# Eight-core decoder trunk: the second token pair's input in eight parts during the first down projection, its norm in the second gate/up, modulation rows paused there, the start modelled with 295 GB/s

## The chip, the cores and the metric

The kernel runs on all 8 cores of one Trainium2 chip, one program for all, each core with one sequence of the batch. The metric is the device time of the slowest core in microseconds (us), over several executions. Cores 0 to 3 are one die, cores 4 to 7 the other. For every execution the span of each core and its mean granted TensorE clock are known (1.0 is full speed); a profile exists for one execution of each kernel.

Executions differ. In most, all cores are within some 10 us of one another. In others some cores run at a lower granted clock and take longer (in the first profile here 1960.5 to 1963.5 us at a mean clock of 0.968 to 0.970, beside 1931.2 to 1935.7 us at 0.985 to 0.990); such cores always came in pairs here, (0,1), (2,3), (4,5) or (6,7), one pair or two. I call an execution **undisturbed** when it is below 1950 us, **short episode** when its slowest core is between 1950 and 2010 us, and **long episode** above 2040 us; nothing lies between 2010 and 2040. Long episodes come with the kernel before and with most of the others here, and no time difference is explained with them. Many short episodes count as "fast" in the ratios (they are within 1.5% of the fastest run), others as slow; I therefore list executions singly where it matters.

## The reference

Two layers, each of three sub-layers (SwiGLU, token mixer, SwiGLU), every one behind an RMSNorm with a shift, scale and gate from a conditioning vector. Only the first SwiGLU matters here (shortened):

```python
D_MODEL = 1024; BATCH = 8; SEQ = 2048; DEPTH = 2; D_FF = 2816
def modulate(x, g, mod):
    shift, scale, gate = jnp.split(mod, 3, axis=-1)
    return rmsnorm(x, g) * (1.0 + scale[:, None, :]) + shift[:, None, :], gate[:, None, :]
def swiglu(h, w_in, w_out):
    g, u = jnp.split(h @ w_in, 2, axis=-1)
    return (jax.nn.silu(g) * u) @ w_out
def reference(...):
    c_act = jax.nn.silu(c)
    for l in range(DEPTH):
        mod = c_act @ w_mod[l] + b_mod[l]               # the "modulation rows"
        h, gate = modulate(x, norm_g[l, 0], mod_f1)
        x = x + 0.5 * gate * swiglu(h, w_ffn_in[l, 0], w_ffn_out[l, 0])
        ...                                             # mixer, second SwiGLU
    return rmsnorm(x, final_g)
```

## The kernel before

The kernel is generated: a scheduler in Python simulates five engines and one shared DMA wire, gives every operation a modelled start, and each engine's program is its operations in the order of these starts. (`L465` in the views is the line of the helper that records every operation, so go by the names of the tiles.) At the end, VectorE, ScalarE and TensorE are ordered once more by `relist`, a list schedule by due time.

The sequence of 2048 tokens is four tiles of 512 (`X[:, t]`), worked on in two pairs. A phase is one sub-layer for one pair; the SwiGLU's 22 blocks of 128 hidden channels go in two groups (12 and 10): gate/up, down, gate/up, down. Weights stream through six slots (`SLOTS`) in pieces of 512 KB. The matrices are multiplied by a scheme with 7 instead of 8 products, which needs sums of weight blocks: VectorE makes them when a piece has landed.

```python
    def piece_sums(pc):                      # VectorE: four sums per weight piece
        ...
        tt_(v(4), v(3), v(2), ALU.add, [k(2), k(3)], [k(4)], half=True)
        tt_(v(3), v(0), v(3), ALU.subtract, [k(0), k(3)], [k(3)], half=True)
        ...
    def rows_pump():                         # one modulation row per 8 ticks, if VectorE has slack
        row_tick[0] += 1
        if row_tick[0] >= ROW_EVERY and slack():
            ...
    Sd.BW = 320e3                            # modelled bandwidth of the start, bytes/us
    ...                                      # start: CT, SM, CB, 12+4 rows, X of the first pair, norm
    for n in range(WARM):                    # WARM = 36: matmuls on idle TensorE at the start
        op = mm(PS[5][:], ONES[:], SQ[:, n % NSQ, :], True, True, ...)
        op.after = 28.0 + n * 0.6
    ...
    Sd.BW = Sched.BW                         # the rest is modelled with another figure
    ...
    def late_x():                            # X of the second pair: two loads of 2 MB
        for t in range(2, 4):
            add("sp", I("dma_start", out=X[:, t, :, :], in_=xT[t]...), reads=[("A", ablk(6, 0))], ..., dma=("X", t))
    ...
                if k == 0 and g == 0:        # first gate/up of the first phase
                    run_segs(segs[:X_AT])    # X_AT = 55
                    late_x()
                    bg_add(stats_gen([2, 3]))    # squares and their sums over channels, for the norm
                    run_segs(segs[X_AT:-3])
                ...
                if g == 0:                   # at the start of the down projection
                    late_norm = pm is not None
                    rstd(other, after=Sd.tl["pe"].tail())   # the norm's roots
                ...
                if not last:
                    run_down(dn, rest)
```

## Time and profile before

| kernel before, first chip | us |
|---|---|
| time, median of 3 executions | 1965.8 (1965.01 to 1966.27) |
| profiled execution: cores 2 to 5 | 1931.2 to 1935.7 |
| profiled execution: cores 0, 1, 6, 7 | 1960.5 to 1963.5 |

The prediction below shows the spans, the slices and the chain. Two more views of core 7 belong to it. TensorE's waits over the whole run (what it waited for; us in total, times, longest):

```profile
PE ps L465 <- ACT SQ L465: 24.9, 2, 19.6
PE ps L465 <- DMA ACTB<-wmod: 4.3, 1, 4.3
PE ps L465 <- DVE TP L465: 3.7, 1, 3.7
```

The first two belong to the start, before there is anything to multiply. The third, one wait of 3.7 us at 123.5 us, is the only large one in the remaining 1900 us. The DMA transfers issued from 105 to 140 us (count, size of one, median us from issue to landing):

```profile
X<-xT SPq DMA_DIRECT2D x2, 2048.0 KB, 19.4
SLOTS<-wout POOLq DMA_DIRECT2D x4, 512.0 KB, 16.1
```

Pieces of down weights (`wout`) that land in 5.3 us in the median of the whole run take 16.1 us beside the two loads of X.

### The profile page before, as it was taken

The page shows a single profiled execution, that of the slowest core. Times are in us where ns is not written, and L with a number is a line of the kernel's source. Part 1 is how long each engine was busy: PE and PEld are TensorE (multiplying, and loading weights), DVE is VectorE, ACT ScalarE, POOL GpSimd, SP SyncE. Part 2 cuts the span into 40 slices and gives each one's busy share as a digit, 9 for nine tenths or more (in the row PEclk, how much of TensorE's full clock was granted, in tenths as well). Part 3 has the DMA queues.
Part 4 walks back from the last instruction along what each step waited for, and adds up shares of the span by engine and source line. Part 5 has one row for each costly group of instructions (what it writes and reads, how often), then busy time and mean ns, then how long its engine had stood idle before and what let it go on. Part 6 is the DMA issues. An engine that isn't in the chain of part 4 may idle for free.

```text
span 1963.5 us, 25398 instructions; the slowest of 8 cores (1931.2 to 1963.5 us)
## 1 busy us (share of the span) xinstructions
PE 1909.8 (97%) x8706; PEld 861.4 (44%) x8706; DVE 1697.0 (86%) x3256; ACT 1031.9 (53%) x1738; POOL 172.4 (9%) x330
## 2 busy tenths in 40 slices
PE   3999999999999999999999999999999999999997
PEld 1534444444444444444444444444444444444443
DVE  4778889999798999999988888898998889988865
ACT  4454455456564555565455544564466555574343
POOL 0000000000202000000000000000000000000000
PEclk6898889999999999999999999999999999999999
DMA  9795748787777768686855454555454444445752
GB/s 271 148 222 121 151 87 182 145 178 155 155 167 175 160 150 183 144 171 122 182 100 89 82 90 77 96 96 87 75 90 67 85 85 86 76 76 86 174 87 94
DMA packets 66653, 248.72 MB, mean 127 GB/s; under 512 B 7520, under 2 KB 7648, under 8 KB 66016
## 3 DMA queue, kind: packets, MB, share of 16 engines
q0 software_dynamic: 42192, 153.64, 46.9%
q1 hardware_dynamic: 24336, 93.45, 14.7%
q8 instruction: 74, 1.21, 0.2%
q14 instruction: 51, 0.42, 0.1%
HBM read 392.29 MB, written 8.39 MB: 204 GB/s over the span
## 4 chain that ended last, share of the span: by engine, by line
PE 91%; DMA 4%; DVE 3%; ACT 1%; SPq 1%; issue 0%; DVEq 0%; POOLq 0%
PE ps L465 91%; DMA ACTB<-wmod 2%; DMA SLOTS<-wout 1%; DVE X L465 1%; SPq L465 1%; DMA SLOTS<-win 1%; DVE WMOD L465 0%; DVE ACTB L465 0%; DVE TP L465 0%; DVE SLOTS L465 0%; ACT PMH L465 0%; ACT ps L465 0%; DVE ps L465 0%; ACT L465 0%; ACT TP L465 0%
## 5 line engine op out<-in xcount | busy, mean ns | idle before, releaser
L465 PE MATMUL ps<-H,SLOTS 128*128 128x512 f16 x5440 | 1214.9, 383 | 9.0 <-DVE TP L465 3.7
L465 PEld LDWEIGHTS ps<-H,SLOTS 128*128 128x128 f16 x5440 | 534.5, 99 | 667.5 <-issue 71.6
L465 ACT ACTIVATE ps<-ps 128x512 f32<-128x512 f32 x684 | 397.8, 582 | 595.0 <-PE ps L465 558.4
L465 PE MATMUL ps<-ACTB,SLOTS 128*128 128x512 f16 x2780 | 628.5, 385 | 0.3
L465 PEld LDWEIGHTS ps<-ACTB,SLOTS 128*128 128x128 f16 x2780 | 274.9, 99 | 339.4 <-issue 46.6
L465 DVE TENSOR_TENSOR SLOTS<-SLOTS 128x512 f16<-128x512 f16 x996 | 393.4, 417 | 17.5 <-DMA SLOTS<-wout 7.7
L465 DVE SCALAR_TENSOR_TENSOR X<-ps,GH,X 128x512 f32<-128x512 f32 x424 | 308.3, 744 | 49.5 <-PE ps L465 45.5
L465 ACT ACTIVATE TP<-ps 128x512 f32<-128x512 f32 x400 | 238.2, 596 | 131.9 <-PE ps L465 130.1
L465 DVE TENSOR_TENSOR ACTB<-TP,ps 128x512 f16<-128x512 f32 x368 | 248.1, 683 | 43.1 <-PE ps L465 28.5
L465 ACT ACTIVATE SQ<-X 128x512 bf16<-128x512 f32 x224 | 131.2, 623 | 103.6 <-DVE X L465 55.3
L465 POOL DMA_DIRECT2D SLOTS<-win x176 | 93.1, 530 | 1047.1 <-PE ps L465 971.5
L465 DVE TENSOR_TENSOR TP<-ps,TP 128x512 f32<-128x512 f32 x176 | 120.9, 687 | 55.0 <-ACT ps L465 54.0
L465 DVE SCALAR_TENSOR_TENSOR WMOD<-WMOD,CB 128x1024 f32<-128x1024 f32 x130 | 157.6, 1216 | 1.9 <-DMA WMOD<-wmod 1.8
L465 DVE TENSOR_TENSOR TP<-X,RS 128x512 f32<-128x512 f32 x192 | 128.5, 683 | 11.4 <-ACT ACTB L465 8.3
L465 DVE TENSOR_TENSOR ps<-ps,TP 128x512 f32<-128x512 f32 x176 | 122.2, 694 | 16.0 <-PE ps L465 15.2
L465 DVE TENSOR_TENSOR ACTB<-ACTB 128x1024 f16<-128x1024 f16 (+1 forms) x188 | 104.2, 564 | 1.4
L465 POOL DMA_DIRECT2D SLOTS<-wout x88 | 46.5, 528 | 516.9 <-PE ps L465 516.9
L465 PE MATMUL ps<-SQ,ONES 128*128 128x512 bf16 x166 | 58.9, 438 | 28.9 <-ACT SQ L465 24.9
L465 ACT ACTIVATE H<-TP,MODT,AS 128x512 f16<-128x512 f32 x81 | 62.9, 807 | 20.7 <-DVE TP L465 13.8
L465 ACT ACTIVATE PMH<-TP,MODT,AS 128x512 f16<-128x512 f32 x60 | 47.7, 807 | 19.1 <-DVE TP L465 19.0
L465 ACT ACTIVATE ACTB<-TP,MODT,AS 128x512 f16<-128x512 f32 x51 | 40.9, 809 | 14.9 <-PE ps L465 12.0
L465 DVE TENSOR_TENSOR SQ<-SQ 128x1024 bf16<-128x1024 bf16 (+1 forms) x56 | 36.3, 647 | 11.9 <-ACT SQ L465 11.5
(74 smaller groups left out, 538.7 us busy)
## 6 DMA issues: line engine op xcount, KB each, us to landing
SLOTS<-win POOLq DMA_DIRECT2D x176, 512.0 KB, 6.2
WMOD<-wmod SPq DMA_DIRECT2D x131, 512.0 KB, 5.5
SLOTS<-wout POOLq DMA_DIRECT2D x88, 512.0 KB, 5.3
SLOTS<-wab POOLq DMA_DIRECT2D x28, 512.0 KB, 8.9
X<-xT SPq DMA_DIRECT2D x4, 2048.0 KB, 21.0
outT<-X SPq DMA_DIRECT2D x16, 512.0 KB, 3.7
ACTB<-wmod SPq DMA_DIRECT2D x13, 512.0 KB, 28.2
CB<-cb SPq DMA_DIRECT2D x1, 512.0 KB, 6.1
```

Of the source, the lines that this page charges most:

```text
L465: return lambda E: getattr(E, name)(*a, **k)
```

## The change

The intent, read from the diff: load X of the second pair where there is more room, in parts that follow TensorE's progress; make its norm where it does not stand in the way; keep VectorE and DMA free of modulation rows in the meantime; and model the start with 295 instead of 320 GB/s. The whole diff:

```diff
--- before.py
+++ after.py
@@ -21,7 +21,7 @@
 EPS = 1e-6
 NSLOT = 6
 STAGE = True
-X_AT = 55
+R_AT = 21
 WARM = 36
 SLG = (2, 3, 4, 6, 7, 7)
 
@@ -843,12 +843,13 @@
 
     row_queue = []
     row_tick = [0]
+    rows_on = [True]
     ROW_EVERY = 8
     SLACK = 3
 
     def rows_pump():
         row_tick[0] += 1
-        if row_tick[0] >= ROW_EVERY and slack():
+        if row_tick[0] >= ROW_EVERY and rows_on[0] and slack():
             row_tick[0] -= ROW_EVERY
             while row_queue and row_queue[0] in done_rows:
                 row_queue.pop(0)
@@ -1489,7 +1490,7 @@
 
 
 
-    Sd.BW = 320e3
+    Sd.BW = 295e3
     add("sp", I("dma_start", out=CT[:], in_=ct_d), writes=["CT"], cost=0.06, dma="CT", nbytes=128 * 32)
     add("sp", I("dma_start", out=SM[:], in_=small_d), writes=["SM"], cost=0.06, dma="SM", nbytes=128 * SM_N * 4)
     add("sp", I("dma_start", out=CB[:], in_=cb_d), writes=["CB"], cost=0.06, dma="CB", nbytes=128 * 4096)
@@ -1614,9 +1615,15 @@
     carry = []
 
     def late_x():
+
         for t in range(2, 4):
-            add("sp", I("dma_start", out=X[:, t, :, :], in_=xT[t].rearrange("p (c k) -> p c k", k=TT)), reads=[("A", ablk(6, 0))],
-                writes=[Xk(c, t) for c in range(NC)], cost=0.06, dma=("X", t), nbytes=128 * 16384)
+            for c in range(0, NC, 2):
+                last = max(o.idx for o in Sd.ops[-60:] if o.eng == "pe")
+                op = add("sp", I("dma_start", out=X[:, t, c:c + 2, :], in_=xT[t][:, c * TT:(c + 2) * TT].rearrange("p (c k) -> p c k", k=TT)),
+                         writes=[Xk(c, t), Xk(c + 1, t)], cost=0.06, dma=("X", t, c), nbytes=128 * 4096, after=Sd.tl["pe"].tail())
+                op.deps.add(last)
+                yield
+                yield
 
     def run_segs(segs, side=iter(())):
 
@@ -1644,6 +1651,7 @@
         nxt = PHASES[k + 1] if k + 1 < len(PHASES) else None
         other = [2, 3] if p == 0 else [0, 1]
         t_begin = Sd.tl["pe"].tail()
+        rows_on[0] = True
         if sub[0] == "F":
             l, i = sub[1], sub[2]
             s = 2 * i
@@ -1663,11 +1671,12 @@
                 segs = [f for _, f in gu_segments(units)]
                 first, rest = dn.segments(segs[-3:])
                 late = last and late_norm
-                if k == 0 and g == 0:
-                    run_segs(segs[:X_AT])
-                    late_x()
-                    bg_add(stats_gen([2, 3]))
-                    run_segs(segs[X_AT:-3])
+                if k == 0 and g == 1:
+                    run_segs(segs[:R_AT])
+                    bg_drain()
+                    rstd(other, after=Sd.tl["pe"].tail())
+                    bg_add(early_h(sub, nxt))
+                    run_segs(segs[R_AT:-3])
                 else:
                     run_segs(segs[:-3])
                 if not late:
@@ -1680,7 +1689,10 @@
                     bg_drain()
                     rstd(other, after=Sd.tl["act"].tail())
                 pm = {("F", 1, 0, 1): 0, ("F", 1, 1, 0): 1}.get(sub + (p,)) if g == 0 else None
-                if g == 0:
+                if g == 0 and k == 0:
+                    late_norm = False
+                    rows_on[0] = False
+                elif g == 0:
                     late_norm = pm is not None
                     rstd(other, after=Sd.tl["pe"].tail())
                 if pm is not None:
@@ -1694,8 +1706,10 @@
                 if g == 0 and nxt is None:
                     bg_add(final_gen(0))
                 if not last:
-                    run_down(dn, rest)
-                    if not late_norm and nxt is not None and STAGE:
+                    run_down(dn, rest, late_x() if k == 0 else iter(()))
+                    if k == 0:
+                        bg_add(stats_gen([2, 3]))
+                    elif not late_norm and nxt is not None and STAGE:
                         carry.append(lambda sub=sub, nxt=nxt: bg_add(early_h(sub, nxt)))
                 elif nxt is not None:
                     run_down(dn, rest, side)
```

## The prediction

> **What bounds the kernel now.** I read the spans of the cores first, because the time is that of the slowest core; then the page's forty slices; then TensorE's waits; then a timeline and stretches of 2 us around the one place that stood out. The cores:
>
> ```profile
> core 4: 1935.7 us, clock 0.990
> core 5: 1933.5 us, clock 0.985
> core 6: 1961.4 us, clock 0.968
> core 7: 1963.5 us, clock 0.970
> ```
>
> Cores 0, 1, 6 and 7 take 1960.5 to 1963.5 us, cores 2 to 5 take 1931.2 to 1935.7 us, with the same program. The page (core 7) says what the work is:
>
> ```profile
> PE   3999999999999999999999999999999999999997
> PEclk6898889999999999999999999999999999999999
> PE 91%; DMA 4%; DVE 3%; ACT 1%; SPq 1%; issue 0%; DVEq 0%; POOLq 0%
> ```
>
> TensorE is full from the second slice to the last but one, and is 91% of the chain. So only three things can shorten the run: less idle time of TensorE, a higher clock, or an earlier start. The clock is below full at the start and in slices 3 to 6 (98 to 295 us). Core 7 there, in stretches (columns: TensorE busy, weight loads, VectorE, ScalarE, GpSimd, granted clock, DMA share, GB/s):
>
> ```profile
> 100.00:120.00 20.00, 20.00 (x95) 9.09 (x93) 19.08 (x41) 9.63 (x17) 1.58 (x3) 1.00 0.97 209
> 120.00:140.00 20.00, 16.28 (x67) 6.66 (x66) 11.54 (x25) 10.65 (x21) 1.06 (x2) 0.89 1.00 262
> 140.00:160.00 20.00, 19.78 (x76) 7.87 (x75) 16.70 (x34) 13.37 (x24) 1.05 (x2) 0.81 0.61 139
> 280.00:300.00 20.00, 20.00 (x81) 8.43 (x80) 16.73 (x32) 5.47 (x10) 1.05 (x2) 0.85 0.49 105
> ```
>
> Between 120 and 140 us TensorE loses 3.7 us, DMA is at 1.00, and from about 137.7 us the clock is 0.81 until about 296.3 us; then it is 1.00 to the end. Core 5 shows 1.00 in all four of these stretches. [...] What happened at 120 to 128 us, in the timeline of core 7:
>
> ```profile
> 111.14 0.53 POOL L465 DMA_DIRECT2D SLOTS<-wout  x1 [5.52 <-PE ps L465]
> 111.39 0.81 SPq L465 DMA_DIRECT2D X<-xT  x2
> ...
> 126.09 0.42 DVE L465 TENSOR_TENSOR SLOTS<-SLOTS 128x512 f16<-128x512 f16 x1 [5.13 <-DMA SLOTS<-wout]
> 126.44 0.68 DVE L465 TENSOR_TENSOR TP<-ps,TP 128x512 f32<-128x512 f32 x1
> ...
> 127.26 9.83 PE L465 MATMUL ps<-H,SLOTS 128*128 128x512 f16 x37 [3.72 <-DVE TP L465]
> ```
>
> The two 2 MB tiles of the second pair are issued at 111.39 us. The piece of down weights issued 0.25 us before takes 14.9 us to land (the page's median is 5.3). VectorE, in order, sits 5.13 us before the first weight sum of that piece; the addition behind it is what TensorE waits for. So the load starves the weights, VectorE passes the wait on, and TensorE stops. On cores 0, 1, 2, 6 and 7 the clock then falls to 0.50 for some 5 us; on core 7 it is back at 1.00 by 132 us, and 0.81 follows some 6 us later.
>
> [...] the eight cores ran dense at 1.00 from 68 to 122 us and again from 296 us to the end, and only one episode of 159 us came, on the cores 0, 1, 6, 7. It looks like an answer to the restart, not to the load. [...]
>
> **The change, part by part.**
>
> *Load of X.* The two 2 MB transfers at 111 us go; eight of 512 KB come during the first down projection, one for two products, issued as TensorE advances. A product is 6 matmuls of 0.213 us (94 in 20 us at full clock), 1.28 us, so a part comes each 2.6 us. At 324 GB/s (93.45 MB of that queue in 14.7% of the span) a part takes 1.6 us of all DMA engines: a share of 0.6 for 20 us. The rows that are paused there took 512 KB in some 7 us, a share of 0.23. The unthrottled core 5 has a mean DMA share of 0.73 from 150 to 200 us, so the sum is about 1.1 for 20 us in the first two thirds of the down, where few weight pieces are released, then less. Landing times will rise to perhaps 10 us; weights loaded there are for the gate/up after it, over 20 us away. I expect no stall of TensorE.
>
> What is saved: the sum of (length minus busy time x clock) in stretches of 2 us from 118 to 148 us is 5.5 us on core 2, 3.1 on core 3, 3.7 on core 4, 3.4 on core 5; on core 7 it is 6.2 up to 132 us. If the stall goes, so does the restart, and I expect the 29.7 us on the four cores to go with it.
>
> *Norm.* The 16 squares (0.62 us) now fall in the down, where ScalarE has only some ten copies of 0.58 us to make. Their order on ScalarE leaves each part about 9 us from its issue to the copy behind it, so a landing up to 9 us holds up nothing. The roots (two of 0.72, two of 0.6 us, two table loads of 1.28) move from the start of the down, where no SiLU is wanted, into the second gate/up. Together about 5.2 us in which no SiLU can run, with TensorE's banks held meanwhile: my estimate is 0 to 2 us of TensorE wait.
>
> *Rows.* None are made from the first down to the end of the first phase; they are made up in the next phase, where VectorE has little room (busy 48.7 of 50 us from 300 to 350 us on core 5, though overlapping records overstate that). The instruction order shows the same 50 rows loaded before the mixer starts. The scheduler puts them behind what TensorE waits for: 0 to 1 us.
>
> *Start.* The modelled bandwidth of the start is 295 instead of 320 GB/s. No transfer changes, but orders do. Of the 36 warming matmuls, 14 stood behind the late row (TensorE waits 4.3 us for it, then runs at clock 0.50 without a gap up to the first real matmul at 63.8 us); now 10 do. Each costs 0.38 us there: 4 x 0.38 = 1.5 us earlier on every core.
>
> *Sum.* Cores 2 to 5: 1935.6 - 5.5, 1931.2 - 3.1, 1935.7 - 3.7, 1933.5 - 3.4 give 1930.1, 1928.1, 1932.0, 1930.1. Core 7: 1963.5 - 29.7 - 6.2 = 1927.6. The slowest less the start's 1.5 us: 1930.5; plus about 1 us for the norm and the rows: 1931.5. The timed figure was 1.5 us above the span in the profiled execution (1965.01 and 1963.5): 1933.
>
> **Rivals.** (a) The limit is tripped anyway, by the hot start or by the denser DMA in the down: for it speaks that no one knows what trips it; against it, that the start at 66 us ramped all cores up with no such answer. Then about 29 us stay on some cores: 1933 + 29 = 1962 at most, some 1957 where the stall's own cost falls away. I give this 0.22. (b) The root block in the gate/up stops TensorE for over 3 us, with a cold clock after it: 3 to 6 us, or a new trip. For it: six banks and a SiLU in each unit; against: copies run in between and the scheduler counted the block. (c) The eight parts delay a weight piece as before, now at the turn to the second gate/up: 2 to 4 us. Against: issue is spread by TensorE's progress. (d) The start gains more than I count: if TensorE stayed warm through the late row, the chain behind it (14.3 us at half clock) would shrink by up to some 5 us, and the time would be 1927. Against: core 6 waited only 2.6 us for that row and still ran at 0.50.
>
> **Range and chances.** No trip and 1925 to 1940: about 0.75. Trip, 1952 to 1963: 0.22. For 8 in 10 the range has to reach into the second: 1924 to 1959. Faster by over 2% means below 1926.5, which takes 6.5 us more than I can find: 0.14. Slower by over 2%: 0.01.
>
> **What would show it.** In the new profile: no wait of TensorE over 1 us after the start; weight landings of at most some 10 us; clock 1.00 on all cores from about 67 us on, and cores within 5 us of one another. The first real matmul near 62.3 us on core 7. I am wrong if 0.81 appears with no stall before it (then the load, not the restart, trips the limit), if the clock falls after the root block near 210 us, or if the cores start much earlier.

"The limit", there and below, is only a name for the granted clock of 0.81; what imposes it was not shown. The working of the 29.7 us used the clock to more digits than the traces give; from the traces it is an estimate of 158.6 us (137.7 to 296.3) x 0.19 = 30.1 us, or 29.3 to 30.9 for a clock of 0.805 to 0.815, and core 7's sum becomes 1927.2 instead of 1927.6. The forecast itself comes from core 4, 1935.7 - 3.7 = 1932.0, less 1.5, plus 1, is 1931.5, and 1933 as timed. Two readings are put right here: on cores 0, 1, 2, 6 and 7 the clock of 0.50 lasted 3.3 to 3.4 us (stretches of 0.5 us), not some 5; and of the eight cores at 1.00 from 68 to 122 us core 4 had 0.99, with TensorE busy for 53.3 of the 54 us.

## The result and the profile after

| | before | after |
|---|---|---|
| time, median of 4 executions each | 1966.03 us | 1937.55 us (1935.16 to 1940.84) |
| ratio after/before, 95% interval | | 0.9857 (0.984 to 0.9874) |
| profiled execution, slowest core | 1963.5 us | 1933.5 us |

The result is correct against the reference. All ratios are the mean time of one kernel's fast runs over that of the other's fast runs of the same rounds, so not quite the ratio of the medians quoted. This is 1.4% faster. The time is 4.6 us above the prediction (1933), inside its range; the profiled execution is the fastest of the four (1935.16).

The spans after (profiled execution):

```profile
core 3: 1933.5 us, clock 0.993
...
core 6: 1932.5 us, clock 0.986
core 7: 1927.7 us, clock 0.993
```

The two groups of cores are gone. Core 7 is 35.8 us shorter than before, core 3 is 2.3 us longer. From the page of core 3, the slices of the granted clock and the chain that ended last:

```profile
PEclk9899999999999999999999999999999999999999
...
PE 88%; DMA 4%; DVE 3%; ACT 2%; SPq 1%; issue 1%; POOL 0%; DVEq 0%
```

After the start the clock is at full: from 68 us to 1900 us every core has a mean of 1.00 in stretches of 56 us and more, and no core has a stretch at 0.81. Two of the stretches of core 7 that the prediction shows (the same columns), now:

```profile
120.00:140.00 20.00, 20.00 (x94) 9.08 (x93) 19.11 (x43) 9.30 (x16) 1.59 (x3) 1.00 0.80 189
140.00:160.00 20.00, 20.00 (x94) 9.11 (x93) 17.56 (x34) 5.60 (x10) 1.05 (x2) 1.00 0.88 199
```

94 matmuls in 20 us at clock 1.00, against 67 and 76 before. And the timeline of core 7 there, where the kernel before had 5.13 us of waiting on VectorE and 3.72 us on TensorE:

```profile
120.78 0.69 DVE L465 TENSOR_TENSOR TP<-ps,TP 128x512 f32<-128x512 f32 x1
...
124.39 0.75 DVE L465 TENSOR_TENSOR SLOTS<-SLOTS 128x512 f16<-128x512 f16 x2
```

No wait stands behind either line. But a second thing differs, and the prediction had not looked for it: the addition (`TP<-ps,TP`, which frees a bank for TensorE) now stands *before* the weight sums (`SLOTS<-SLOTS`). In the kernel before it stood behind one, at 126.44. What did it: the missing load, or the order?

The new places. The parts of X lie in the first down projection; transfers of core 3 issued from 145 to 190 us:

```profile
X<-xT SPq DMA_DIRECT2D x7, 512.0 KB, 10.4
SLOTS<-win POOLq DMA_DIRECT2D x7, 512.0 KB, 10.6
WMOD<-wmod SPq DMA_DIRECT2D x5, 512.0 KB, 12.1
```

The load is thinner but the weights and rows beside it are late (`win` lands in 5.7 us and `wmod` in 5.9 us in the median of the whole run), and on some cores this reaches TensorE. Core 5, timeline (the bracket is the engine's idle time before the line, and what ended it):

```profile
163.87 0.42 DVE L465 TENSOR_TENSOR SLOTS<-SLOTS 128x512 f16<-128x512 f16 x1 [5.26 <-DMA SLOTS<-win]
...
165.10 10.52 PE L465 MATMUL ps<-ACTB,SLOTS 128*128 128x512 f16 x48 [2.10 <-DVE X L465]
...
208.90 3.40 PE L465 MATMUL ps<-H,SLOTS 128*128 128x512 f16 x15 [0.59 <-DVE ps L465]
```

VectorE sits 5.26 us before a weight sum whose piece is late, and the update of X behind it holds up TensorE for 2.10 us: the old mechanism on a smaller scale, at another place. The last line is all that the norm's roots cost in the second gate/up. On core 3, a modulation row does the same:

```profile
186.37 1.22 DVE L465 SCALAR_TENSOR_TENSOR WMOD<-WMOD,CB 128x1024 f32<-128x1024 f32 x1 [3.13 <-DMA WMOD<-wmod]
...
188.35 1.02 PE L465 MATMUL ps<-H,SLOTS 128*128 128x512 f16 x4 [1.98 <-DVE TP L465]
```

The pause is not complete: from 145 to 290 us core 3 still makes 9 rows, against 19 in the kernel before and 16 without the pause (experiment 3); 5 of the 9 lie before 190 us.

### The profile page after: what moved, and what is told of

It reads as the page before. It is cut to its first block, busy times and chain, and to the rows that moved or that the text cites. A ratio compares the mean times of both kernels' runs of the same rounds, so it can differ in the third digit from the quotient of the medians.

```text
span 1933.5 us, 25425 instructions; the slowest of 8 cores (1927.7 to 1933.5 us)
## 1 busy us (share of the span) xinstructions
PE 1880.4 (97%) x8706; PEld 853.4 (44%) x8706; DVE 1694.7 (88%) x3256; ACT 1030.3 (53%) x1738; POOL 174.6 (9%) x330
## 4 chain that ended last, share of the span: by engine, by line
PE 88%; DMA 4%; DVE 3%; ACT 2%; SPq 1%; issue 1%; POOL 0%; DVEq 0%
PE ps L465 88%; DMA WMOD<-wmod 3%; DMA SLOTS<-win 1%; SPq L465 1%; DVE WMOD L465 1%; DVE SLOTS L465 1%; DVE ACTB L465 1%; DVE TP L465 1%; DVE X L465 0%; ACT ps L465 0%; ACT PMH L465 0%; DVE ps L465 0%; ACT ACTB L465 0%; ACT TP L465 0%; ACT L465 0%
## 5 line engine op out<-in xcount | busy, mean ns | idle before, releaser
L465 PE MATMUL ps<-H,SLOTS 128*128 128x512 f16 x5440 | 1199.7, 379 | 9.3 <-ACT ps L465 3.3
L465 PE MATMUL ps<-ACTB,SLOTS 128*128 128x512 f16 x2780 | 613.8, 379 | 0.1
```

The lines of the kernel that those rows point to most:

```text
L465: return lambda E: getattr(E, name)(*a, **k)
```

## The experiments

My theory after the result was that of the prediction: the 4 MB load makes the stop, the stop makes the restart, and the restart trips the 0.81 limit. Rivals: the limit is tripped by something else (the load itself, or chance), and another part of the change removed the stop. Twelve runs of ten kernels were made, on four further chips, called B, C, D and E here; all gave correct results. Each kernel was timed against the kernel before on its chip, except `stall8` (one look).

### 1. Only the start's modelled bandwidth (chip B)

```diff
 # kernel before
-    Sd.BW = 320e3
+    Sd.BW = 295e3
```

> The kernel before with only the start's modelled bandwidth changed (295 instead of 320 GB/s). My theory (the start gains 1.5 us, the rest comes from the stall at 122 to 127 us and the limit that follows it): first real matmul on core 7 near 62.1 us instead of 63.8, the stall and the 0.81 episode of some 159 us remain, 1964 us. Rival (the start is what matters): no episode, about 1938 us.

Measured: 1935.85 us median of 5 executions; four at 1934.9 to 1935.9, one at 1963.31 with cores 6 and 7 long. Ratio 0.9911 (0.9819 to 1.0003; the interval is wide because executions of before with short episodes count as fast). The expectation fell. X is still two loads of 2 MB at 110.84 us, and `wout` pieces still land late, in 15.3 us in the median; yet core 7 has no stop of TensorE (the longest wait there on any core is 0.90 us):

```profile
120.68 0.69 DVE L465 TENSOR_TENSOR TP<-ps,TP 128x512 f32<-128x512 f32 x1
...
124.53 0.76 DVE L465 TENSOR_TENSOR SLOTS<-SLOTS 128x512 f16<-128x512 f16 x2 [0.16 <-DMA SLOTS<-wout]
```

The addition stands before the weight sums, as in the changed kernel. The order of the program was changed by nothing but a modelled time of the start. So the start's "no transfer changes, but orders do" had a consequence 60 us later that the prediction had not looked at.

### 2. All of the change but the start's bandwidth (chip B)

```diff
 # changed kernel
-    Sd.BW = 295e3
+    Sd.BW = 320e3
```

> The changed kernel with the start's modelled bandwidth as before (320 GB/s). My theory: no stall over 2.5 us at 120 to 200 us, clock 1.00 after 68 us on all cores, only the start comes 1.7 us later: 1939 us. Rival (the start is what matters): the episode is back, about 1965 us.

Measured: 1939.2 us median of 4 (1936.12, 1938.13, 1940.27, and one long episode, 2188.37). Ratio 0.992 (0.9763 to 1.0076), by itself unclear. As expected: no stop at 124 us and no short episode. The order is still the old one, the sum ahead of the addition, but with no load of X beside it the piece is there in time (`wout` lands in 7.4 us in the median from 105 to 140 us); core 7:

```profile
121.27 0.41 DVE L465 TENSOR_TENSOR SLOTS<-SLOTS 128x512 f16<-128x512 f16 x1
121.60 0.68 DVE L465 TENSOR_TENSOR TP<-ps,TP 128x512 f32<-128x512 f32 x1
```

TensorE waits at most 0.74 us there on any core (core 1). So the two halves of the change each remove the stop, one by moving the load, the other by accident of order. The expected limit of 2.5 us for stalls up to 200 us did not hold, nor the clock of 1.00: the waits in the down are larger here, and core 3 shows 0.71 from 190 to 194 us (4 matmuls take 1.02 us at 190.46 us and 1.86 us at 191.66 us):

```profile
188.48 1.23 DVE L465 SCALAR_TENSOR_TENSOR WMOD<-WMOD,CB 128x1024 f32<-128x1024 f32 x1 [3.93 <-DMA WMOD<-wmod]
...
190.46 1.02 PE L465 MATMUL ps<-H,SLOTS 128*128 128x512 f16 x4 [3.86 <-DVE TP L465]
```

### 3. The change without the pause of the rows (chip B)

```diff
 # changed kernel
-                    rows_on[0] = False
```

> The changed kernel with the modulation rows not paused. My theory: some 20 rows more before 300 us, DMA in the first down at 1.00 for longer, TensorE's waits there grow from about 2 us to 2 to 4 us, and no episode [...]: 1938 to 1943 us. Rival (the pause is what removes the stall): a stall of 4 us or more in the down and the 0.81 episode back, about 1968 us.

Measured: 1946.78 us median of 4 (1943.69, 1945.57, 1947.98, and one long episode, 2262.37). Its undisturbed executions average 1945.7 us, against 1939.6 us of the undisturbed ones of before on this chip (ratio by all fast runs 0.9964). In the profile cores 0, 2, 4 and 6 take 1941.2 to 1946.4 us, the other four 1933.2 to 1935.3. Core 0:

```profile
188.25 1.23 DVE L465 SCALAR_TENSOR_TENSOR WMOD<-WMOD,CB 128x1024 f32<-128x1024 f32 x1 [7.58 <-DMA WMOD<-wmod]
...
194.05 0.58 PE L465 MATMUL ps<-H,SLOTS 128*128 128x512 f16 x1 [7.53 <-DVE TP L465]
```

A row that lands late stops VectorE for 7.58 us, and TensorE for 7.53. The expected 2 to 4 us of waits and 1938 to 1943 us were too low. All eight cores have a second wait that no row makes; core 1:

```profile
252.99 18.33 PE L465 MATMUL ps<-ACTB,SLOTS 128*128 128x512 f16 x75 [3.17 <-ACT ps L465]
```

ScalarE's copy, for which TensorE waits here, now stands behind five operations of the next norm (`H<-TP`): another change of order that a switch brought along. The changed kernel has no such wait. So the pause is worth some 8 us as a whole (1945.7 here; `no_bw` averages 1938.2 on this chip, the changed kernel 1937.8 on the first chip and 1936.5 on chip D, undisturbed), but not by sparing rows alone, and how the 8 us divide was not tested. The stops at 190 us, 5.16 to 7.53 us on four cores, slowed TensorE down there (core 0: weight loads 0.43 us apart from 195.03 to 198.87 us, 8 in 1.61 us before the stop; on cores 2, 4 and 6 the next 115 matmuls took 26.22 to 27.53 us, and the 108 behind them 23.47 us) and were followed by no short episode in three undisturbed executions (one of them profiled).

### 4. A stop of 3.7 us put into the changed kernel (chips B and D)

```diff
 # changed kernel; the eight operations have a modelled cost of 0.05 us, so no order changes
+    op = add("pool", I("tensor_scalar", out=SCR[:, 0:64], in0=CB[:, 0:64], scalar1=1.0, ...), ...)   # x8
+    first_matmul_of_segment_62.deps.add(op.idx)      # k == 0, g == 0
```

> The changed kernel with a stop put in on purpose: one matmul of the first gate/up, near 118 us, waits for a chain of eight small GpSimd operations, an estimated 3 to 5 us in which TensorE stands still on all cores at once, with no more DMA than before. My theory (the restart after a stop trips the limit): 0.81 for about 159 us on at least four cores some 10 us later, about 1965 to 1970 us. Rival (the limit needs the saturated DMA beside the matmuls): only the stop is lost, clock 1.00 afterwards, about 1942 us.

(The 3 to 5 us in it are an estimate that fits the profile before, where GpSimd's operations on `STAT` took 307 and 693 ns each: eight of them 2.5 to 5.5 us.)

Measured, one execution on chip B: 1967.37 us, with cores 2 and 3 at 1960.9 and 1965.8 and the other six at 1934.6 to 1940.0: the time as expected, the limit on two cores instead of "at least four". Core 2, the stop in the timeline, and then stretches (columns as before; granted clock third from the end):

```profile
124.39 15.82 PE L465 MATMUL ps<-H,SLOTS 128*128 128x512 f16 x62 [3.74 <-POOL SCR L465]
```

```profile
124.00:128.00 4.00, 3.61 (x10) 1.40 (x11) 0.69 (x1) 1.09 (x2) 0.24 (x1) 0.60 0.45 139
128.00:132.00 4.00, 4.00 (x20) 1.75 (x18) 3.71 (x10) 1.51 (x3) 0.58 (x1) 0.98 0.32 28
132.00:138.00 6.00, 6.00 (x29) 2.64 (x27) 5.64 (x12) 2.73 (x6) 0.53 (x1) 0.96 0.81 189
138.00:296.00 158.00, 157.82 (x601) 65.32 (x602) 124.43 (x235) 77.67 (x132) 10.61 (x20) 0.81 0.60 122
```

This is the kernel before over again: a low clock (0.60 from 124 to 128 us), nearly the full one (0.98 and 0.96 up to 138 us), and from 137 to about 296 us 0.81; the first part of X is issued only at 151.58 us. To count, the same kernel ran again with repetitions:

> The changed kernel with the stop of 3.7 us at 124 us, made by eight GpSimd operations, again, to count: if a restart at that place trips the limit by itself, a third or more of the executions have a pair of cores about 28 us longer (near 1967), as the kernel before; if the one execution seen was chance, none or one in six, and the rest give 1938 to 1942.

Measured on chip D: 1944.84, 1989.15, 1971.72, 1981.7, 1943.1, 1968.06 us: four short episodes in six, each on one or two pairs. With the first, five of seven. The changed kernel itself, in the same rounds, had one in six. So a stop at that place does bring the episode in most executions, and not in all. (Only the first execution has a trace of an episode; the other four are counted by their length, and their start was not seen.) Both undisturbed executions are 1943 and 1945 us: the stop by itself costs 6 to 8 us there (3.7 us idle, and then a clock of 0.50 to 0.78 from 124 to 128 us on seven of eight cores and 1.00 on core 6, in the profiled one; how much of the 6 to 8 us the clock makes was not taken apart).

### 5. Only the order on VectorE (chip C)

```diff
 # kernel before, after the last ordering: the sum that waits for the late piece goes behind
 # the five operations (addition, products to ACTB, ...) that it stood ahead of
+    i = next(n for n, o in enumerate(dve) if n > 160 and o.swap and waits_for_slot_0(o))
+    dve[i].start = dve[i + 5].start + 1e-4
```

One operation moves on VectorE; the other engines' programs are identical.

> The kernel before with one change: on VectorE the one weight sum that waits for the slow piece of down weights stands behind the five operations (one addition, two ScalarE-fed updates and their like) that it stood ahead of; X is still two 2 MB loads at about 111 us. Theory A (VectorE's order makes the stop of TensorE, and the restart after the stop can trip the 0.81 limit): TensorE's wait of 3.7 us at about 123.5 us falls below 1 us, the piece still lands about 15 us after its issue, no core shows 0.81, all executions in the normal state give about 1936 to 1938. Theory B (the 4 MB load itself, by its traffic, trips the limit): some executions still have a pair of cores some 28 us longer and give about 1964, as in about half of the executions of the kernel before.

Measured: 1936.92 us median of 6: five at 1934.98 to 1938.49, one long episode (2088.26), no short one. The kernel before, 11 executions in the same rounds: six at 1937.02 to 1940.14, three short episodes (1968.57, 1984.48, 1994.03), two long ones. Ratio of fast runs 0.999 (0.9977 to 1.0004): undisturbed executions gain 1.9 us in the mean, and not even that is certain. Core 7:

```profile
111.70 1.32 SPq L465 DMA_DIRECT2D X<-xT  x2
...
121.05 0.69 DVE L465 TENSOR_TENSOR TP<-ps,TP 128x512 f32<-128x512 f32 x1
...
124.50 0.75 DVE L465 TENSOR_TENSOR SLOTS<-SLOTS 128x512 f16<-128x512 f16 x2
```

And the piece's landing is as slow as ever; transfers issued from 105 to 140 us:

```profile
X<-xT SPq DMA_DIRECT2D x2, 2048.0 KB, 17.3
...
SLOTS<-wout POOLq DMA_DIRECT2D x5, 512.0 KB, 14.3
```

TensorE waits at most 0.54 us there on any core (core 6). So with this order the slow landing was harmless. With experiment 2, where the old order was harmless without the slow landing, it follows that the stop needs both: the late piece, and the sum placed ahead of work TensorE needed.

### 6. X in eight parts over the first gate/up instead (chip C)

```diff
 # kernel before, with Sd.BW = 295e3; the norm where it was, no pause of rows
-                    run_segs(segs[:X_AT])
-                    late_x()
+                    run_segs(segs[:6])
+                    run_segs(segs[6:X_AT], late_x())      # the eight parts, one for six segments
```

> The kernel before with the start's modelled bandwidth of the change (295) and X of the second pair in eight 512 KB parts over the first gate/up, from its 7th segment on and one for six segments; the norm where it was, no pause of the rows. If the waits of 1.2 to 2.1 us that the changed kernel has in the first down come from its eight parts there, they are gone here, and the time is 2 to 4 us below the changed kernel: 1932 to 1935. If the parts delay weight pieces of the first gate/up instead (it is close behind the start, where DMA is full), a wait of 2 to 5 us comes there, and the time is 1936 to 1942.

Measured: 1934.79 us median of 6 (1933.49 to 1935.13), no episode of either kind; ratio 0.9979 (0.9965 to 0.9993). DMA behind the start was full only in part (core 0: a share of 0.96 from 62 to 66 us, 0.64 from 70 to 80, 1.04 from 110 to 120). The parts land in 10.4 us on core 3, as in the changed kernel, and TensorE has no wait over 0.36 us on any core from 66 to 140 us, and none of 0.3 us from 150 to 250 us. So the waits of the changed kernel in the down come from what it put there, the parts of X and the norm's squares. It is below the changed kernel by 2 to 3 us, by the undisturbed averages of different chips (1934.6 against 1937.8 and 1936.5).

### 7. A shorter stop, and a later one (chips C and E)

```diff
 # changed kernel
-    eight operations, k == 0, segment 62
+    stall4: four operations, same place
+    stall_late: eight operations, k == 4, segment 62
```

> The changed kernel with four small GpSimd operations that one matmul of the first gate/up waits for, so TensorE stops for about half as long as in the run with eight (3.7 us there): about 1.9 us at 124 us on all cores. If any stop can trip the limit: a pair of cores is some 28 us longer in some executions (about 1964). If the stop has to be longer than that (the clock has to fall first): no 0.81, all normal executions at 1937 to 1940.

Measured: the stop was 2.72 us, not 1.9 (from 2.72 and 3.73 us for four and eight, an estimate of 0.25 us for one operation and 1.7 us that do not depend on their number). 1941.3 and 1942.56 us undisturbed, and two long episodes (2088.2, 2184.74); no short one. The clock fell on cores 0 and 3 only (0.61 from 124 to 128 us, 1.00 on the others), which are two of eight, while after 3.7 us it fell on all eight in the first profile of `stall8` (0.50 to 0.67 in the same stretch). Two undisturbed executions out of four say nothing on whether 2.7 us can trip the limit: inconclusive. The length alone does not decide it: in the profile of the kernel before, core 6 stopped for 2.08 us and core 0 for 2.62, and both fell to 0.50 and then 0.81, while core 5 stopped for 2.34 us and core 4 for 2.28 and stayed at 1.00.

> The changed kernel with the stop of 3.7 us that eight GpSimd operations make, at the same place of a later phase (about 1000 us) instead of the first gate/up. If a restart of all cores at the same time trips the limit wherever it comes: 0.81 on a pair of cores from about 1005 us for some 160 us, about 1967 in some of the executions. If only the stretch just after the start can be tripped: no 0.81, and 1940 to 1943 (the 3.7 us of the stop alone).

> The changed kernel with the stop of 3.9 us at 730 to 735 us (the first run of it had been announced for about 1000 us, which was a wrong estimate of the phase's place) again, to count beside the stop at 124 us, after which five of seven executions had a pair of cores about 28 us longer. If a stop anywhere trips the limit as often: four of six executions near 1968. If only a stop close behind the start does: none or one of six, the others at 1940 to 1946.

The announced 1000 us was wrong: TensorE restarts at 730 to 735 us in the first run and 730 to 739 us in the second, after 3.92 us on every core. First, on chip C: 1940.62 to 1945.44 us in four executions, no episode. Again, on chip E: 1944.94, 1943.76, 2047.24, 2172.02, 2001.44, 1970.58: two short episodes and two long ones in six. The profiles caught undisturbed executions; in the first run's the clock fell there (to 0.50 to 0.74 in the lowest stretch of 4 us of each core), and nothing followed (1.00 on all cores from 760 to 900 us). Core 0, first run:

```profile
736.00:740.00 4.00, 4.00 (x11) 1.37 (x9) 1.98 (x3) 0.58 (x1) 0.00 (x0) 0.50 0.19 78
...
744.00:900.00 156.00, 155.80 (x720) 70.14 (x721) 150.32 (x300) 87.08 (x147) 13.60 (x26) 1.00 0.70 145
```

Two of ten, against five of seven at 124 us. This leans to "only close behind the start", but neither expectation came out cleanly, and where the two episodes began is not known. One difference: at 124 us the cores restart within 1.1 us of one another (first profile of `stall8`), at 730 us within 5 us (first run; 9 us in the second). Open.

### 8. The changed kernel again, and a version with fewer warming matmuls (chip D)

> The changed kernel again, beside the kernel before on one more chip. Theory A (the order on VectorE makes a stop of TensorE, and a restart after a stop may trip the 0.81 limit on a pair of cores): 1935 to 1941 in every execution, no pair 28 us longer; the kernel before gives 1937 to 1941 in some executions, of which the changed kernel saves only 1 to 3 us, and 1964 or more in the others. If the gain of the first measurement (28 us) is there in every execution: all executions of the kernel before at 1964 to 1967, ratio about 0.986.

Measured: 1938.16 us median of 6: 1934.32, 1935.29, 1937.42, 1938.9, one short episode (1982.86), one long (2122.47). Before, 11 executions: nine at 1937.64 to 1941.54, one short (1975.27), one long. Ratio of the fast runs **0.9987** (0.9973 to 1.0001). Of the 28 us of the first measurement 2.4 us are left (1938.9 to 1936.5), and the interval just reaches 1. "No pair 28 us longer" was too strong: one in six had two pairs some 30 to 50 us longer.

```diff
 # spread
-WARM = 36
+WARM = 24
```

> The kernel spread (eight parts over the first gate/up) with 24 warming matmuls of the start instead of 36: the last twelve, of which five or six stand behind the late row at half clock for 0.38 us each, are gone. If those only delay: the first real matmul 2 us earlier, 1932 to 1933. If they keep the clock up there: TensorE stays at half clock for longer, and the time is 1935 to 1938.

Measured: undisturbed 1932.94, 1934.0 and 1934.33 us; the other three executions were long episodes (2068 to 2195), all with the die of cores 4 to 7. Ratio of the fast runs 0.9975 (0.9957 to 0.9993). The first real matmul is at 62.19 us on core 3, against 62.87 in `spread`: 0.7 us, not 2. In its undisturbed executions it is 2.7 us below the changed kernel on the same chip, the best measured here, but that rests on three executions.

### The count

| kernels | executions | undisturbed | short episode | long episode |
|---|---|---|---|---|
| before, first chip | 4 | 0 | 4 | 0 |
| before, chips B, C, D, E | 40 | 24 | 10 | 6 |
| no stop at 124 us: changed, 1, 2, 5, 6, `spread_w24` | 37 | 29 | 2 | 6 |
| stop of 3.7 us at 124 us (`stall8`) | 7 | 2 | 5 | 0 |
| stop of 3.9 us at 730 us | 10 | 6 | 2 | 2 |

Left out are `rows_on` (3 undisturbed, 1 long) and `stall4` (2 and 2), whose stops are elsewhere or shorter. Episodes are counted by length alone; where one began is known for two profiles only, before and `stall8`.

Long episodes are about as common in the kernel before (6 of 44) as without the stop (6 of 37). Short ones are not: 14 of 44 in the kernel before, 5 of 7 with a stop put in, 2 of 37 without. But it is chance in each execution, and it varies from chip to chip (4 of 4 on the first, 1 of 11 on chip D).

## Why the prediction was right or wrong

**The time** was right: 1937.55 us for 1933, in range. That the kernel before stood at 1965.8 beside it was luck: on chip D the same pair of kernels differs by 2.4 us.

**What bounded the kernel before.** That the time was the 0.81 stretch on four cores is confirmed: they lost about 32 us (core 7: 35.8), cores 2 to 5 between nothing and 6.6 (core 3 became 2.3 us longer). What I took for a property of the kernel was an event of this execution: 24 of 40 executions of the same kernel on other chips do not have it. One profiled execution and three nearly equal times made it look fixed: all four executions of before in the first comparison were short episodes, and none of the changed kernel's.

**"So the load starves the weights, VectorE passes the wait on, and TensorE stops."** The first half holds. The second is the step that fell short: VectorE passed the wait on only because one sum stood ahead of the addition. With that one operation moved the load stays, the landing stays at 14.3 us, and the stop is gone (experiment 5). The load is needed as well: with the old order and no load there is no stop either (experiment 2). I had seen the line `SLOTS<-SLOTS [5.13]` directly above `TP<-ps,TP`, and had not asked why it stood there.

**"If the stall goes, so does the restart, and I expect the 29.7 us on the four cores to go with it."** The direction holds: a stop made of operations without use brings the episode back in five of seven executions, in the one that was profiled with the same 0.81 and the same end near 296 us (experiment 4). But it is a matter of chance, not of rule, and without the stop it still came in 2 of 37.

**"It looks like an answer to the restart, not to the load"** is supported for the place at 124 us: `stall8` has the stop without the load, and `swap` and `bw_only`, which keep the load without the stop, had one short episode in 11 executions (at the rate of the kernel before, 14 of 44, it would be 3 or 4, so this half is thin by itself). Why a restart trips it in one execution and not in the next is open, and so is whether it needs the nearness of the start: the stops of `rows_on` at 190 us tripped nothing.

**Start: 1.5 us.** The first real matmul of core 7 came at 62.11 us instead of 63.82, 1.7 us; right. That the same line also changes the order at 124 us was not foreseen: alone it gave 1935.4 us (mean of the undisturbed executions) for 1939.6 on its chip, 4.2 us.

**Load of X: "I expect no stall of TensorE."** Wrong by 1 to 2 us on some cores: 2.10 us on core 5, 1.60 on core 0, 1.20 on core 6, 1.25 and 1.98 on core 3. The landing of 10.4 us was estimated well ("perhaps 10"), the conclusion from it was not: the weights loaded there have VectorE's sums waiting for them in front of other work. Rival (c), on a small scale.

**Norm: 0 to 2 us.** 0.59 us of waiting on core 5. Right.

**Rows: "0 to 1 us".** As a cost, not contradicted: core 6 has a wait of 1.84 us at 699 us behind a late row, but `spread`, which has no pause, has one of 2.48 us there on core 1. As a judgement of the part, incomplete: I had not asked what happens without the pause. It is some 8 us longer (experiment 3). "None are made" was wrong: core 3 makes 9 rows from 145 to 290 us, and a late one of them is behind the wait of 1.98 us.

**Sum.** I predicted 1930.1, 1928.1, 1932.0 and 1930.1 us for cores 2 to 5 before the corrections of -1.5 and +1, so 1929.6 in the mean; they have 1929.0, 1933.5, 1930.4 and 1931.3, 1931.05 in the mean. The 1.5 us between match the waits in the down (0.61 us on core 2, 3.23 on core 3, 2.10 on core 5: 1.5 in the mean), and core 3 is now the slowest. One term was misread: the 6.2 us of core 7 up to 132 us are 5.4 by the same formula; core 7 did not set the forecast. And between undisturbed executions the whole change is worth 2.4 us (chip D), where the forecast for the slowest of cores 2 to 5 was 4.2 (1935.7 to 1931.5); where the rest stays is open, since no undisturbed execution of the kernel before has a profile. The landing time of 14.9 us (5.3 in the median) shows only that the piece was late beside X; how the DMA engines share their time between the two was not shown.

## What to carry to other kernels

Here a late transfer alone did not stop TensorE (`swap`: landing in 14.3 us, no wait over 0.54 us), nor did an unlucky order alone (`no_bw`: no wait over 0.74 us); what stopped it was VectorE waiting for the transfer with needed work behind it. Look at what stands behind each wait before moving the load, and compare instruction orders even where a change touches only a modelled figure. And before a gain of 1 to 2% is credited to a change, run the kernel before often, on more than one chip: here 28 us of the first measurement were an event that 24 of 40 executions elsewhere do not have. What the change itself brings is some 2 us, hardly clear of the noise, and a smaller chance of that event.
